# Splitting 128 rows per partition 64/64 instead of 65/63 in a two-group gate-and-dispatch kernel

## The chip, the cores and the metric

The kernel runs on one core of one Trainium2 chip. The metric is the device time of one execution in microseconds (us). Six runs of the kernel before gave a median of 240.24 us, from 240.06 to 240.39.

## The reference

For each of 16 x 1024 = 16,384 tokens there are eight router logits and a row of 512 floats (2 KB). The two largest softmax probabilities are taken and normalised against each other, and the row is written out twice, once multiplied by the smaller and once by the larger of the two weights:

```
probs = softmax(router_logits)
topk_indices = argsort(probs)[..., -2:]
topk_probs = take(probs, topk_indices);  topk_probs /= sum(topk_probs)
out = (x repeated k=2 times) * topk_probs[..., newaxis]     # [16, 1024, 2, 512] float32
```

So 33.55 MB of x and 0.52 MB of logits are read, and 67.11 MB of output are written. After normalising, the two weights are the sigmoids of minus and plus the difference of the two largest logits.

## The kernel before

The 16,384 tokens are put on 128 partitions, 128 tokens (called rows here) for each. They are cut into two groups by `GROUPS`: in the first, each partition has 65 successive rows of x, in the second 63. In the memory of the chip's DRAM the rows of one partition lie together, so neighbouring partitions are 65 x 2 KB = 130 KB apart in x and 65 x 4 KB = 260 KB apart in the output for the first group, and 126 KB and 252 KB for the second.

Three tiles in SBUF matter. `xs` has room for one group of rows (65 slots of 2 KB for each partition). `osp` holds the output of 16 rows (16 x 4 KB). `logits` holds all logits. `WA` holds both weights of each row.

For each group the SyncE queue (SP) first issues the loads of `LOADS[g]`, in rows: 2, 4, 2, 8, 17, 28, 4 for the first group and 16, 16, 31 for the second. The logits are loaded after the first six rows, and VectorE (DVE) works out the weights (lines 24 to 40, with two sigmoids on ScalarE in lines 42 and 43). Then a list named `plan` is worked through. Each entry is a first row, a number of rows and a place for the output; one multiplication on DVE (line 128) writes both copies, and one DMA (line 136) stores them. The entries of a group are:

- the first 16 rows into `osp` (in the first group as 2 rows, stored from ScalarE's queue, and 14 rows);
- rows 16 to 31 into slots 0 to 31 of `xs`, over rows that are no longer needed;
- rows 32 to 39 and 40 to 47 into the two halves of `osp`;
- the entries of `LAST[g]`, written over slots of `xs`: rows 48 to 56 and 57 to 64 in the first group, rows 48 to 62 in the second. The function `over` puts the output of row r into slots 2r - G and 2r - G + 1, where G is the number of rows of the group. For row 48 and G = 65 that is slot 31.

Everything on SP is in one order: the loads of group 0, the stores of group 0, the loads of group 1, the stores of group 1. A transfer that has to wait holds up all that stands behind it on SP. The framework puts in the waits: a load into slots of `xs` waits for the stores that read them, and a multiplication waits for the loads that it reads and for the stores that read what it overwrites.

A DMA over 128 partitions is shared by 16 DMA engines, eight partitions for each. In the trace's packet records each partition's stretch of a DMA is one packet: a store of 16 rows has 128 packets of 64 KB, a load of 28 rows 128 packets of 56 KB.

Of the kernel before, what the change touches and what calls it, by code (L numbers as in the profile page):

```python
# [1 line left out]

# [4 lines left out]

F32 = mybir.dt.float32
ALU = mybir.AluOpType
ACTF = mybir.ActivationFunctionType  # L10
P = 128


def top2_weights(nc, pool, logits, M, E, tag=""):

    hi, lo, n = None, None, E  # L20
    while n > 1:
        n //= 2
        if hi is None:
            a, b = logits[:, :, 0:n], logits[:, :, n : 2 * n]
            nhi = pool.tile([P, M, n], F32, tag=f"hi{n}{tag}")
            nlo = b
            nc.vector.tensor_tensor(nhi, a, b, op=ALU.max)  # L27
            nc.vector.tensor_tensor(nlo, a, b, op=ALU.min)  # L28
        else:
            a, b = hi[:, :, 0:n], hi[:, :, n : 2 * n]  # L30
            nhi = pool.tile([P, M, n], F32, tag=f"hi{n}{tag}")
            nlo = pool.tile([P, M, n], F32, tag=f"lo{n}{tag}")
            tmp = pool.tile([P, M, n], F32, tag=f"tmp{n}{tag}")
            nc.vector.tensor_tensor(tmp, lo[:, :, 0:n], lo[:, :, n : 2 * n], op=ALU.max)  # L34
            nc.vector.tensor_tensor(nlo, a, b, op=ALU.min)  # L35
            nc.vector.tensor_tensor(nlo, nlo, tmp, op=ALU.max)  # L36
            nc.vector.tensor_tensor(nhi, a, b, op=ALU.max)  # L37
        hi, lo = nhi, nlo
    dlt = pool.tile([P, M], F32, tag=f"dlt{tag}")
    nc.vector.tensor_tensor(dlt, hi[:, :, 0], lo[:, :, 0], op=ALU.subtract)  # L40
    WA = pool.tile([P, M, 2], F32, tag=f"WA{tag}")
    nc.scalar.activation(WA[:, :, 0], dlt, ACTF.Sigmoid, scale=-1.0)  # L42
    nc.scalar.activation(WA[:, :, 1], dlt, ACTF.Sigmoid, scale=1.0)  # L43
    return WA

GROUPS = [65, 63]

LOADS = [[2, 4, 2, 8, 17, 28, 4], [16, 16, 31]]


LAST = [[(48, 9), (57, 8)], [(48, 15)]]


@with_exitstack
def kernel(
    ctx: ExitStack,
    tc: tile.TileContext,  # L60
    x: bass.AP,
    router_logits: bass.AP,
    k: bass.AP,
    out: bass.AP,
):
    nc = tc.nc
    B, S, D = x.shape
    E = router_logits.shape[-1]
    N = B * S
    assert int(k) == 2 and E == 8 and N == P * sum(GROUPS)  # L70
    M = N // P

    L = 16
    x_v, o_v, rl_v = [], [], []
    t0 = 0
    for n in GROUPS:
        t1 = t0 + P * n
        x_v.append(
            x.rearrange("b s d -> (b s) d")[t0:t1].rearrange("(p m) d -> p m d", p=P)
        )  # L80
        o_v.append(
            out.rearrange("b s k d -> (b s) k d")[t0:t1].rearrange(
                "(p m) k d -> p m k d", p=P
            )
        )
        rl_v.append(
            router_logits.rearrange("b s e -> (b s) e")[t0:t1].rearrange(
                "(p m) e -> p m e", p=P
            )
        )  # L90
        t0 = t1

    wpool = ctx.enter_context(tc.tile_pool(name="wpool", bufs=1))
    logits = wpool.tile([P, M, E], F32)
    xs = wpool.tile([P, max(GROUPS), D], F32)
    osp = wpool.tile([P, L, 2, D], F32)

    def over(r, n, G):

        a = 2 * r - G
        return xs[:, a : a + 2 * n, :].rearrange("p (r k) d -> p r k d", k=2)

    h = L // 2
    e = 2
    m0 = 0
    for g, G in enumerate(GROUPS):
        r = 0  # L110
        for n in LOADS[g]:
            nc.sync.dma_start(xs[:, r : r + n, :], x_v[g][:, r : r + n, :])  # L112
            r += n
            if g == 0 and r == 6:

                nc.sync.dma_start(logits[:, :G], rl_v[0])  # L116
                nc.sync.dma_start(logits[:, G:], rl_v[1])
                WA = top2_weights(nc, wpool, logits, M, E)
        assert r == G
        begin = [(0, e, osp[:, :e]), (e, L - e, osp[:, e:])] if g == 0 else [(0, L, osp)]  # L120
        plan = begin + [
            (L, L, over(L, L, 2 * L)),
            (2 * L, h, osp[:, :h]),
            (2 * L + h, h, osp[:, h:]),
        ]
        plan += [(r, n, over(r, n, G)) for r, n in LAST[g]]
        for r, n, og in plan:
            nc.vector.tensor_tensor(  # L128
                og,
                xs[:, r : r + n, :].unsqueeze(2).to_broadcast([P, n, 2, D]),  # L130
                WA[:, m0 + r : m0 + r + n, :].unsqueeze(3).to_broadcast([P, n, 2, D]),
                op=ALU.mult,
            )

            queue = nc.scalar if n == e else nc.sync
            queue.dma_start(o_v[g][:, r : r + n], og)  # L136
        m0 += G


# [1 line left out]
_INS = ['x', 'router_logits', 'k']  # L141
_OUTS = [((16, 1024, 2, 512), 'float32')]

_NUMBERS = {'k': 2}


# [26 lines left out]
```

## Time and profile before

| What | Value |
|---|---|
| Median of six runs | 240.24 us (240.06 to 240.39) |
| The profiled execution's own time | 240.09 us |
| Its span in the profile | 238.3 us, so 1.8 us lie outside of it |
| DVE busy | 142.0 us (60%) |
| DMA moved | 101.19 MB, mean 425 GB/s |
| Busy share of the 16 DMA engines | 97.8% for SP's queue (q1) and 1.0% for ScalarE's (q10) |

The span is cut into 40 slices, and a digit gives the busy share of a slice in tenths. A "wait" row says which instruction waited, on what, for how long. SP is not a computing engine here; "SPq" is its queue of issues. The figures of the DMA share are sums of packet times as a share of 16 engines' span.

### The profile page before, as it was taken

To read this page: it belongs to the slowest core of one execution; us is meant where nothing else is said; L and a number is where in the kernel's file an instruction comes from. 1 tells how busy PE (TensorE), PEld (TensorE's weight loads), DVE (VectorE), ACT (ScalarE), POOL (GpSimd) and SP (SyncE) were. 2 spreads that over 40 slices of the span, in tenths; PEclk is the share of its full clock that TensorE was granted. 3 is DMA by queue.
4 is the path that set the end of the run, shared out by engine and by line. 5 is a ranking of instruction groups with operands and counts; after the bars stand their busy time and mean duration, and the time that the engine had idled before them with its cause. 6 is when DMAs were issued, how large, how long until landed. Compare 5 with 4: busy or idle time off the path is not lost.

```text
span 238.3 us, 117 instructions
## 1 busy us (share of the span) xinstructions
DVE 142.0 (60%) x23; ACT 1.8 (1%) x3; POOL 0.2 (0%) x4
## 2 busy tenths in 40 slices
DVE  0599999900299699900000699999106999990000
ACT  2000000000000000000000000000000000000000
POOL 0000000000000000000000000000000000000000
DMA  6999999899798999999999999998998989999995
GB/s 250 435 481 386 446 488 462 330 462 462 341 517 352 440 440 440 440 402 478 434 429 423 402 506 405 448 484 385 429 451 385 495 352 440 440 440 429 495 443 217
DMA packets 3456, 101.19 MB, mean 425 GB/s; under 512 B 384, under 2 KB 512, under 8 KB 896
## 3 DMA queue, kind: packets, MB, share of 16 engines
q1 hardware_dynamic: 3312, 100.14, 97.8%
q10 hardware_dynamic: 144, 1.05, 1.0%
HBM read 34.08 MB, written 67.11 MB: 425 GB/s over the span
## 4 chain that ended last, share of the span: by engine, by line
DMA 43%; DVE 41%; issue 4%; SPq 1%; ACT 0%; DVEq 0%
DVE xs L128 22%; DVE osp L128 18%; DMA out_dram<-xs 15%; DMA xs<-in_x_dram 13%; DMA out_dram<-osp 13%; DMA logits<-in_router_logits_dram 3%; SPq L112 0%; DVE nhi L27 0%; DVE logits L28 0%; DVE nlo L36 0%; DVE tmp L34 0%; DVE nhi L37 0%; DVE nlo L35 0%; SPq L116 0%; SPq L136 0%
## 5 line engine op out<-in xcount | busy, mean ns | idle before, releaser
L128 DVE TENSOR_TENSOR osp<-xs,WA 128x8192 f32<-128x8192 f32 (+3 forms) x7 | 69.1, 9908 | 61.9 <-DMA xs<-in_x_dram 31.2
L128 DVE TENSOR_TENSOR xs<-xs,WA 128x16384 f32<-128x16384 f32 (+3 forms) x5 | 69.1, 13811 | 2.2 <-DMA out_dram<-xs 2.0
L27 DVE TENSOR_TENSOR nhi<-logits 128x512 f32<-128x512 f32 x1 | 0.7, 692 | 8.3 <-DMA logits<-in_router_logits_dram 8.3
L42 ACT ACT_TABLE_LOAD x1 | 1.3, 1283 | 0.7 <-PEq L154 0.7
L28 DVE TENSOR_TENSOR logits<-logits 128x512 f32<-128x512 f32 x1 | 0.7, 691 | 0.0
L35 DVE TENSOR_TENSOR nlo<-nhi 128x256 f32<-128x256 f32 (+1 forms) x2 | 0.7, 350 | 0.0
L36 DVE TENSOR_TENSOR nlo<-nlo,tmp 128x256 f32<-128x256 f32 (+1 forms) x2 | 0.7, 350 | 0.0
L37 DVE TENSOR_TENSOR nhi<-nhi 128x256 f32<-128x256 f32 (+1 forms) x2 | 0.7, 349 | 0.0
L34 DVE TENSOR_TENSOR tmp<-logits 128x256 f32<-128x256 f32 x1 | 0.4, 417 | 0.0
L42 ACT ACTIVATE WA<-dlt 128x128 f32<-128x128 f32 x1 | 0.3, 315 | 10.2 <-DVE dlt L40 10.2
L40 DVE TENSOR_TENSOR dlt<-nhi,nlo 128x128 f32<-128x128 f32 x1 | 0.3, 292 | 0.0
L43 ACT ACTIVATE WA<-dlt 128x128 f32<-128x128 f32 x1 | 0.3, 299 | 0.0
L34 DVE TENSOR_TENSOR tmp<-nlo 128x128 f32<-128x128 f32 x1 | 0.3, 282 | 0.0
L154 POOL MEMSET const-bfloat16-1.0<- 128x1 bf16 x1 | 0.1, 102 | 0.0
L154 POOL MEMSET const-uint8-127<- 128x1 uint8 x1 | 0.1, 101 | 0.0
L154 POOL MEMSET const-float32-0.0<- 128x1 f32 x1 | 0.1, 99 | 0.2 <-issue 0.2
L154 POOL MEMSET const-float32-1.0<- 128x1 f32 x1 | 0.1, 98 | 0.0
## 6 DMA issues: line engine op xcount, KB each, us to landing
out_dram<-osp SPq DMA_DIRECT2D x4, 4096.0 KB, 20.7
xs<-in_x_dram SPq DMA_DIRECT2D x2, 4096.0 KB, 30.0
xs<-in_x_dram SPq DMA_DIRECT2D x1, 7936.0 KB, 37.8
out_dram<-xs SPq DMA_DIRECT2D x1, 7680.0 KB, 23.1
xs<-in_x_dram SPq DMA_DIRECT2D x1, 7168.0 KB, 39.6
out_dram<-osp SPq DMA_DIRECT2D x1, 7168.0 KB, 33.8
out_dram<-xs SPq DMA_DIRECT2D x1, 4608.0 KB, 20.4
xs<-in_x_dram SPq DMA_DIRECT2D x1, 4352.0 KB, 22.6
```

The costliest lines, as they stand in the source:

```text
L27: nc.vector.tensor_tensor(nhi, a, b, op=ALU.max)
L28: nc.vector.tensor_tensor(nlo, a, b, op=ALU.min)
L34: nc.vector.tensor_tensor(tmp, lo[:, :, 0:n], lo[:, :, n : 2 * n], op=ALU.max)
L35: nc.vector.tensor_tensor(nlo, a, b, op=ALU.min)
L36: nc.vector.tensor_tensor(nlo, nlo, tmp, op=ALU.max)
L37: nc.vector.tensor_tensor(nhi, a, b, op=ALU.max)
L40: nc.vector.tensor_tensor(dlt, hi[:, :, 0], lo[:, :, 0], op=ALU.subtract)
L42: nc.scalar.activation(WA[:, :, 0], dlt, ACTF.Sigmoid, scale=-1.0)
L43: nc.scalar.activation(WA[:, :, 1], dlt, ACTF.Sigmoid, scale=1.0)
L128: nc.vector.tensor_tensor(og, xs[:, r : r + n, :].unsqueeze(2).to_broadcast([P, n, 2, D]), WA[:, m0 + r : m0 + r + n, :].unsqueeze(3).to_b ...
L154: nc = _bacc.Bacc("TRN2", target_bir_lowering=False, num_devices=1)
```

## The change

The two groups get 64 rows each, so neighbouring partitions are 128 KB apart in x and 256 KB apart in the output in both groups. The first group is loaded in pieces of 2, 4, 2, 8, 16 and 32 rows (six instead of seven), the second in 16, 16 and 32. The last 16 rows of each group are one multiplication and one store; with G = 64 their output goes into slots 32 to 63. `xs` has 64 slots instead of 65. The loop is untouched.

```diff
+GROUPS = [64, 64]
 
-GROUPS = [65, 63]
-
-LOADS = [[2, 4, 2, 8, 17, 28, 4], [16, 16, 31]]
+LOADS = [[2, 4, 2, 8, 16, 32], [16, 16, 32]]
 
 
-LAST = [[(48, 9), (57, 8)], [(48, 15)]]
+LAST = [[(48, 16)], [(48, 16)]]
```

## The prediction

> **What bounds the kernel now.** I read the profile's page first: the engines' busy times, the row of DMA shares, the queues.
>
> ```profile
> DVE 142.0 (60%) x23; ACT 1.8 (1%) x3; POOL 0.2 (0%) x4
> ...
> DMA  6999999899798999999999999998998989999995
> ...
> q1 hardware_dynamic: 3312, 100.14, 97.8%
> q10 hardware_dynamic: 144, 1.05, 1.0%
> ```
>
> The reader is to see that no computing engine is near full and that the 16 DMA engines are: 97.8 + 1.0 = 98.8% of 238.3 us is 235.4 us of packets on each. The packet records say where the missing 2.9 us lie: the first data packet starts at 1.97 us and the last one ends at 237.35 us. Those ends are 235.4 us apart, so between them the engines never run dry. The time is therefore the packet time plus 2.9 us at the ends plus the 1.8 us outside the span. The profiled execution took 240.09 us; the median is 0.15 above it. I sum differences on the profiled execution and lay them on the median.
>
> The waits come next, DVE's and SP's, and then the timeline.
>
> ```profile
> DVE osp L128 <- DMA xs<-in_x_dram: 31.2, 1, 31.2
> DVE osp L128 <- DMA out_dram<-osp: 30.1, 2, 16.7
> ...
> DVE xs L128 <- DMA out_dram<-xs: 2.0, 1, 2.0
> ```
>
> ```profile
> SPq L112 <- DMA out_dram<-xs: 20.0, 2, 10.3
> ...
> SPq L112 <- DMA xs<-in_x_dram: 2.4, 2, 2.1
> ```
>
> ```profile
> 64.02 17.30 DVE L128 TENSOR_TENSOR osp<-xs,WA 128x8192 f32<-128x8192 f32 x2 [16.70 <-DMA out_dram<-osp]
> 72.73 8.94 SPq L136 DMA_DIRECT2D out_dram<-osp  x2
> 83.36 18.48 DVE L128 TENSOR_TENSOR xs<-xs,WA 128x9216 f32<-128x9216 f32 x2 [2.05 <-DMA out_dram<-xs]
> 93.14 9.06 SPq L136 DMA_DIRECT2D out_dram<-xs  x2
> ...
> 180.90 17.29 DVE L128 TENSOR_TENSOR osp<-xs,WA 128x8192 f32<-128x8192 f32 x2 [13.40 <-DMA out_dram<-osp]
> ...
> 214.42 0.33 SPq L136 DMA_DIRECT2D out_dram<-xs  x1
> ```
>
> All these waits are of engines waiting for a DMA queue that is full. A wait removed is worth nothing unless the queue would have run dry. So two questions decide: does the packet time change, and does the queue run dry anywhere in the new order?
>
> **Packet time from sizes.** In the packet records a packet's duration depends on its size almost alone. Medians in ns: 8 KB 309, 32 KB 1213, 34 KB 1288, 36 KB 1364, 56 KB 2116, 60 KB 2267, 62 KB 2342, 64 KB 2418. From 32 to 64 KB that is 37.7 ns per KB and 8 ns per packet. Each DMA gives an engine eight packets.
>
> - Removed: loads of 17, 28, 4 and 31 rows (34, 56, 8, 62 KB): 10.30 + 16.93 + 2.47 + 18.74 us. Stores of 9, 8 and 15 rows (36, 32, 60 KB): 10.91 + 9.70 + 18.14 us. Sum 87.19 us.
> - Added: a load of 16 rows (32 KB) 9.70, and two loads of 32 rows and two stores of 16 rows, all of 64 KB packets: 4 x 19.34. Sum 87.08 us.
> - Two DMAs fewer also means two closing packets of 9 ns fewer for each engine, 0.02 us.
>
> Together -0.13 us. Bytes are the same, so nothing else in this term can move. That a load is cut into 64 KB packets is not shown (the largest load packet is 62 KB; 64 KB ones occur in stores); loads and stores of 56 KB have the same median, 2116 ns, so I take the store's figure. Cut in two it would cost 8 x 8 ns more.
>
> **The 4-row load.** One of the removed loads was dearer than its size. The 4-row load at the end of group 0 took a mean of 370 ns per packet, from 309 to 745, between 43.5 and 46.9 us; the other 4-row load, near the start, a mean of 309. The excess is 8 x 61 ns = 0.49 us on each engine, in the path. In the new kernel its rows are part of a 32-row load. The nearest row is the last load of group 1 (31 rows, mean 2345 against 2342), with an excess of 0.02 us. But the cause is not to be seen, and a stutter of DRAM reads at that moment would hit whatever load is running. So the term lies between 0 and -0.48; I take -0.24, since of the two loads with 8 KB packets one had the whole excess and one none.
>
> **The queue in the new order.** Group 0 loads end 0.6 us earlier (64 rows), and all that follows shifts with them; I keep the old clock.
> - DVE's 2.05 us wait at 83.36 existed because row 48's output began in slot 31, which the store of slots 0 to 31 still read. It now begins in slot 32, so the wait goes. DVE runs 64.02 + 17.30 + 17.23 (the 16-row multiplication, from its two rows of 17.22 and 17.23) = 98.6 us until the last store of group 0 is issued, where the first of two pieces was issued at 93.14. The queue needs it at 102.0, when the first packet of the old piece started. Slack 3.4 us, from 8.9.
> - The second load of group 1 waited for that same slot 31 until 113.5; now it goes out at once, behind the first. The third still waits, for the whole last store, to about 122 us, with two loads of 9.7 us queued ahead of the engines. That 19.4 us is the cover; gone, the gap would be about the 1.24 us from the first issue (0.73) to the first packet (1.97). Behind the waiting SP stands only the store issued near 149, so nobody is held up.
> - The last store of all is issued at 180.90 + 17.29 + 17.23 = 215.4 instead of 214.42; its packets are needed at 218.7. Slack 3.3 us, from 4.3.
> - SP's 2.1 us wait before the ninth transfer falls away with that transfer; SP's next issue is at 30.09, so nothing follows.
> - DVE's instruction for 9 and 8 rows (18.48 together) becomes 17.23, its last 16.16 becomes 17.23. Both only use slack.
>
> With 1.24 us from issue to packet the queue stays full. The sum is -0.13 - 0.24 = -0.37 us: 239.72 on the profiled execution, 239.87 on the median. Its own range is 239.63 to 240.11, the two ends of the 4-row term.
>
> **A rule against the change.** Before, partitions lay 130 or 126 KB apart in x and 260 or 252 KB in the output; 128 and 256 KB are powers of two. The trace shows no such pitch. It does show that doubling the pitch, from 130 KB (load of 28 rows) to 260 KB (store of 14 rows), leaves 56 KB packets at 2116 ns, so I put the cost at nothing in the sum. The Trainium skill, "DMA: Bandwidth & Descriptors", section "Latency and other measured facts", says that copies whose partitions lie a large power of two apart in HBM lose rate, 207 GB/s at 512 KiB and 103 at 4 MiB where the padded pitch gives 214. No run here shows it. An estimate by that page: the loss at 512 KiB, 3.3%, would make about 8 us of 235.4; our pitches are smaller by 2 and 4, so less. The sum by the row stays 239.87.
>
> **Rivals.**
> 1. *The power-of-two pitch slows the packets* (slower). For it: 16 engines run nearly in step, so their addresses would differ by multiples of the pitch. Against it: medians and minima of the large packets agree within a few ns, so the engine's own rate sets them, and DRAM has to fall below that before any time is lost. Price by rows: at least nothing; the mildest disturbance seen is the 17-row load beside ScalarE's store, 1297 against 1288 ns (0.7%), the strongest the 4-row load's 370 against 309 (20%). All large packets are the undisturbed kind, so I stay near the mild row: 0.7% of 235.4 is 1.65 us, less 0.37, gives 241.5. It decides as soon as 64 KB packets pass 2432 ns, their largest so far. Chance 0.24.
> 2. *The last store comes too late* (slower). ScalarE's store was issued at 15.09 and its first packet started at 18.86, 3.8 us later, among busy engines. If a store on SP needs as long, slacks of 3.4 and 3.3 us leave gaps of 0.4 and 0.5 us, and with the 0.37 gained the time is 240.8. Against it: that was another queue, which had to fall in behind packets already taken up. It decides where the slack falls below the time from issue to packet. Chance 0.06.
> 3. *The whole excess of the 4-row load goes* (faster): -0.13 - 0.48 gives 239.63. For it, the last load of group 1; against it, the unknown cause. Chance 0.24, with all that lies below 239.76.
>
> The sum's case, with rates as they are and the excess partly back, has the remaining 0.46.
>
> **How the numbers follow.** A measurement can tell about 0.2% here, 0.48 us: faster is below 239.76, slower above 240.72. Faster is rival 3, 0.24. Slower is rivals 1 and 2, 0.30. The rest is 0.46. The range goes down to 239.55, just past rival 3, and up to 242.5, past rival 1's price; the dearer half of the pitch case, about 0.12, is left out above, and 0.05 below.
>
> **What would show it.** Right: DMA share near 98.8%, first packet near 2.0 and no gap inside; 64 KB packets at 2418 ns for loads and stores alike; DVE's wait for the store from xs gone; the third load of group 1 issued near 122. Wrong by rival 1: medians above 2432 and 1213 ns. By rival 2: an idle stretch of the DMA before the last store of a group. By rival 3: last load of group 0 with no packet above its size's median.

## The result: slower by 0.4%

The changed kernel took 241.09 us (median of 18 runs, 240.62 to 242.42), beside 240.26 us (36 runs, 239.96 to 240.90) for the kernel before. The ratio is 1.0039, with a 95% interval of 1.0029 to 1.0048. The forecast was 239.87 us.

The profiled execution of the change took 240.75 us, its span is 239.0 us. It lies 0.34 below its own median, so the profile shows 0.66 of the 0.83 us. The page's rows that answer to those of before, the busy times, the slices and the queues:

```profile
DVE 141.8 (59%) x22; ACT 1.8 (1%) x3; POOL 0.2 (0%) x4
...
DMA  7999998899989799999989998989999898999894
...
q1 hardware_dynamic: 3024, 100.14, 97.8%
q10 hardware_dynamic: 144, 1.05, 1.0%
```

The queue is as full as before, in a longer span: the same bytes took more packet time. DVE's waits, SP's waits and the timeline of the change:

```profile
DVE osp L127 <- DMA xs<-in_x_dram: 33.5, 1, 33.5
DVE osp L127 <- DMA out_dram<-osp: 30.2, 2, 16.2
```

```profile
SPq L111 <- DMA out_dram<-xs: 21.8, 1, 21.8
...
SPq L135 <- DMA xs<-in_x_dram: 2.1, 1, 2.1
```

```profile
63.56 17.30 DVE L127 TENSOR_TENSOR osp<-xs,WA 128x8192 f32<-128x8192 f32 x2 [16.21 <-DMA out_dram<-osp]
...
80.89 17.23 DVE L127 TENSOR_TENSOR xs<-xs,WA 128x16384 f32<-128x16384 f32 x1
98.14 0.33 SPq L135 DMA_DIRECT2D out_dram<-xs  x1
98.53 23.87 SPq L111 DMA_DIRECT2D xs<-in_x_dram  x3
131.62 17.23 DVE L127 TENSOR_TENSOR osp<-xs,WA 128x16384 f32<-128x16384 f32 x1 [33.51 <-DMA xs<-in_x_dram]
...
180.14 17.29 DVE L127 TENSOR_TENSOR osp<-xs,WA 128x8192 f32<-128x8192 f32 x2 [14.03 <-DMA out_dram<-osp]
...
214.72 0.33 SPq L135 DMA_DIRECT2D out_dram<-xs  x1
```

The reader is to see that the order did what was foretold: the row of DVE's wait for a store from `xs` (2.0 us before) is gone; DVE goes from one multiplication to the next at 80.89 with no wait, the last store of group 0 is issued at 98.14, and SP waits once for a store from `xs`, 21.8 us, before the third load. Nor does the queue run dry: the packet records show fewer than 16 packets under way only at the two ends.

Where the time went, from packet records (a packet's *excess* is what it took beyond the median for its size, summed and divided by 16 engines):

| us per engine | before | change |
|---|---|---|
| first load (2 rows) | 0.53 | 0.60 |
| load of rows 16 on, beside ScalarE's store | 0.07 | 0.22 |
| last load of group 0, before its stores | 0.49 | 0.57 |
| last store of group 0, before the loads of group 1 | 0.00 | 0.14 |
| first two loads of group 1 | 0.05 | 0.12 |
| last load of group 1, before its stores | 0.02 | 0.22 |
| all packets | 1.20 | 1.89 |

0.69 us more excess, less the 0.13 us that the sizes save, comes near the 0.57 us by which the stretch from first packet to last grew (235.38 to 235.95 us). The sum is of the mean engine and the slowest one sets the stretch (it ended 0.29 us behind the mean before, 0.38 in the change), so that it comes out so closely is partly chance. 0.13 us more lies behind the last landing (below). The excess does not lie on all packets: medians are 2418 ns for 64 KB, loads and stores alike. Most of it lies where loads and stores meet: on 16 packets, the last of each engine, of the load that ends at 46.2 us, of the store that ends at 121.3, and of the load that ends at 160.4.

(The packet times in the prediction were read against a start 0.23 us too early. The first packet starts at 1.74 us, 1.0 us after its issue, and the slacks were 3.2 and 3.1 us. No step turns on it.)

### The profile page after: what moved, and what is told of

Its sections match the earlier page's. It is cut to its first block, busy times and chain, and to the rows that moved or that the text cites. A ratio compares the mean times of both kernels' runs of the same rounds, so it can differ in the third digit from the quotient of the medians.

```text
span 239.0 us, 112 instructions
## 1 busy us (share of the span) xinstructions
DVE 141.8 (59%) x22; ACT 1.8 (1%) x3; POOL 0.2 (0%) x4
## 4 chain that ended last, share of the span: by engine, by line
DMA 43%; DVE 41%; issue 4%; SPq 1%; ACT 0%; DVEq 0%
DMA out_dram<-osp 27%; DVE osp L127 25%; DVE xs L127 14%; DMA xs<-in_x_dram 14%; DMA logits<-in_router_logits_dram 3%; SPq L111 0%; DVE nhi L27 0%; DVE logits L28 0%; DVE nlo L36 0%; DVE nhi L37 0%; DVE nlo L35 0%; DVE tmp L34 0%; SPq L115 0%; SPq L135 0%; ACT WA L42 0%
## 5 line engine op out<-in xcount | busy, mean ns | idle before, releaser
L127 DVE TENSOR_TENSOR xs<-xs,WA 128x16384 f32<-128x16384 f32 x4 | 68.9, 17225 | 0.1
```

The lines of the kernel that those rows point to most:

```text
L127: nc.vector.tensor_tensor(og, xs[:, r : r + n, :].unsqueeze(2).to_broadcast([P, n, 2, D]), WA[:, m0 + r : m0 + r + n, :].unsqueeze(3).to_b ...
```

## Experiments

The theories at the start: 1, reads 128 KB apart; 2, the sizes of the pieces; 3, stores 256 KB apart. Ratios are to the kernel before on the same chip, with 95% intervals.

**e1: the change with reads 130 KB apart.** The view of x has 65 rows for each partition; 64 are read.

```diff
+        rd = 65
+        c0 = min(t0, N - P * rd)
         x_v.append(
-            x.rearrange("b s d -> (b s) d")[t0:t1].rearrange("(p m) d -> p m d", p=P)
+            x.rearrange("b s d -> (b s) d")[c0 : c0 + P * rd].rearrange(
+                "(p m) d -> p m d", p=P
+            )
```

> The changed kernel, but x is read with 65 rows (130 KB) between partitions in both groups; it reads other rows than the reference wants, as many and in the same pieces; stores stay 256 KB apart. Theory 1 (reads 128 KB apart lose time wherever stores are in flight beside them): the extra time goes, 240.1 us, ratio to the kernel before 0.998 to 1.0005, and the last packets of group 0's 32-row load are back near 2418 ns (they were 2830 to 3212). Theory 2 (64 KB load packets and one-piece stores): stays at 241.1 us, ratio 1.004. Theory 3 (stores 256 KB apart): also stays at 241.1.

Measured 241.03 us, 1.0034 (1.0021 to 1.0047), and 0.65, 0.21 and 0.40 us of excess at the three switches. Theory 1 alone fails.

**e5: the kernel before with reads 128 KB apart.** The view of x has 64 rows for each partition and the load's first row is `min(r, 64 - n)`.

> The kernel before with all its pieces and stores, but x read with 64 rows (128 KB) between partitions (the last row of group 0 is read from one row too low, so that it fits; sizes are as before). Theory 1: slower by what the change cost, 240.9 to 241.2 us, ratio 1.003 to 1.004. Theory 2 and theory 3: 240.26 us, ratio 1.000.

Measured 240.26 us, 1.0004 (0.9992 to 1.0016). Theory 1 fails here too.

**e2: the kernel before with a 32-row load.**

```diff
-LOADS = [[2, 4, 2, 8, 17, 28, 4], [16, 16, 31]]
+LOADS = [[2, 4, 2, 8, 17, 32], [16, 16, 31]]
```

> The kernel before with its last two loads of group 0 (28 and 4 rows) joined to one of 32 rows, so 64 KB load packets at 130 KB between partitions. Theory 1: no loss, 239.8 to 240.3 us; if the 4-row load's 0.49 us was due to its small packets, 239.8, if it belongs to the switch from loads to stores, 240.2. Theory 2: slower, 240.6 us. Theory 3: 240.2.

Measured 240.32 us, 1.0010 (0.9997 to 1.0023). With the 4-row load gone its excess stayed: the 32-row load that took its place has 0.52 us, on each engine's last packet. So the prediction's -0.24 us was nothing: the excess belongs to the switch from loads to stores, whatever packet is there.

**e3: the change with small pieces.** Loads 2, 4, 2, 8, 16, 28, 4 and 16, 16, 28, 4; last pieces of 9 and 7 rows in both groups.

> The changed kernel (64 and 64 rows, 128 and 256 KB between partitions) with small pieces as before: the 32-row loads cut into 28 and 4 rows, the last stores into 9 and 7 rows. Theory 1 and theory 3 (distance between partitions): stays near 241.1 us, ratio 1.004. Theory 2 (sizes): back at 240.3, ratio 1.000.

Measured 241.30 us, 1.0038 (1.0026 to 1.0050): as slow as the change. Theory 2 fails.

**e6: the kernel before with stores 256 KB apart.** The output views have 64 rows for each partition; the last store of group 0 is cut. The lines of the views and the `else` with the old store are left out here ("...").

```diff
...
+            if r + n > 64:
+                queue.dma_start(o_v[0][:, r:64], og[:, : 64 - r])
+                queue.dma_start(o_v[1][:, 63:64], og[:, 64 - r :])
...
```

> The kernel before with its groups, loads and multiplications, but its output rows stored 64 rows (256 KB) apart in both groups; the 65th row of each partition is stored by a DMA of its own into the free place of the second half (output rows stand elsewhere, as many are written). That DMA of 4 KB packets costs 0.06 us by packet sizes. Theory 3 (stores 256 KB apart): 241.0 to 241.3 us, ratio 1.003 to 1.004, with the excess of load packets at the switches between loads and stores in group 1 above 0.2 us. Theory 4 (the distance does not matter, it is the equal split itself: how the pieces' ends fall against each other): 240.3 us, ratio 1.000.

Measured 240.44 us, 1.0008 (1.0000 to 1.0017). The loads at the two switches of group 1 have 0.26 us of excess (0.07 in the kernel before), the sign that theory 3 named, but the time moved by less than it expected.

**e7: the change with stores 260 and 252 KB apart.** As in e6 the other way round: the views are cut at row 65 x 128, and the last row of group 1 goes into the free place of the first view.

> The changed kernel with its groups, loads and multiplications, but its output rows stored 65 rows (260 KB) apart in the first half and 63 rows (252 KB) apart in the second, as in the kernel before; the last row of each partition is stored by a DMA of its own into the free place of the first half (output rows stand elsewhere). It costs 0.06 us by packet sizes. Theory 3: 240.2 us, ratio 0.999 to 1.001, and the excess at the switches in group 1 back under 0.1 us. Theory 4: stays at 241.1 us, ratio 1.004.

Measured 240.80 us, 1.0017 (1.0005 to 1.0029), its runs from 240.10 to 241.40. Half of the loss is gone. The excess at the switches of group 1 did not go as theory 3 expected: the last store's packets are back at their median, but the last load of group 1 has 0.49 us, more than in the change.

**e8: both distances doubled.** One view of 128 rows for each partition, of which a group takes 64. The edit of x is shown; output and logits have the same one ("...").

```diff
-            x.rearrange("b s d -> (b s) d")[t0:t1].rearrange("(p m) d -> p m d", p=P)
+            x.rearrange("b s d -> (b s) d").rearrange("(p m) d -> p m d", p=P)[
+                :, c0 : c0 + n
+            ]
...
```

> The changed kernel with both groups taken from one layout of 128 rows for each partition, so that x is read 256 KB apart and the output is stored 512 KB apart; pieces and order are those of the change. Theory 3: more loss than at 256 KB, above 241.3 us; an estimate by the Trainium skill's 3.3% at 512 KiB would be about 248 us. Theory 4: 241.1 us, as the change.

Measured 242.44 us, 1.0093 (1.0080 to 1.0106). Pieces and order are those of the change, so the distances did it, those of reads and stores together. The timeline says where:

```profile
63.32 17.29 DVE L130 TENSOR_TENSOR osp<-xs,WA 128x8192 f32<-128x8192 f32 x2 [16.08 <-DMA out_dram<-osp]
...
132.75 17.22 DVE L130 TENSOR_TENSOR osp<-xs,WA 128x16384 f32<-128x16384 f32 x1 [34.89 <-DMA xs<-in_x_dram]
...
181.67 17.29 DVE L130 TENSOR_TENSOR osp<-xs,WA 128x8192 f32<-128x8192 f32 x2 [14.43 <-DMA out_dram<-osp]
```

Between the first two rows the queue moves stores of 16, 8, 8 and 16 rows and a load of 16: 19.34 + 9.70 + 9.70 + 19.34 + 9.70 = 67.78 us by sizes. The rows are 69.43 us apart, 1.65 too many; the change's rows of the same kind (63.56 and 131.62) are 0.28 too many. In that stretch lies the one switch from stores to loads, and the packets agree: 1.0 us of excess on the last packets of the store, 0.64 on the first load behind it.

The 3.3% at 512 KiB that the prediction estimated from the Trainium skill's rates for copies between tensors in HBM ("DMA: Bandwidth & Descriptors", "Latency and other measured facts") is not what this kernel pays at that store distance: 0.9%.

**e9: the kernel before with all stores on SP.** Line 135 reads `queue = nc.sync`.

> The kernel before with its first store (2 rows) on SP's queue, behind the loads, instead of ScalarE's, so that no store runs beside the loads of group 0. If the mix of loads and stores costs what the excess of the load packets between 14 and 26 us shows (0.07 us in the kernel before, 0.22 in the changed one): 240.1 to 240.2 us, ratio 0.9995. If the excess at the end of group 0's loads (0.49 us) comes from the first stores to the output in general, it stays there; if it comes from the store on the other queue, it goes: 239.7.

Measured 240.46 us, 1.0008 (1.0000 to 1.0017). The excess of the 17-row load fell from 0.07 to 0.03 us, that of the last load of group 0 stayed at 0.53. So that one does not come from ScalarE's queue, and the mix of queues is not worth removing.

**e10: the change with both distances off the power of two (e1 and e7 together).**

> The changed kernel with its groups and pieces, but both sides off the power of two: x read 130 KB apart, output stored 260 and 252 KB apart, the last row of each partition by a DMA of its own (other rows are read and the output rows stand elsewhere; as many). Theory 5 (reads and stores both count: where one side or the other lies a power of two apart, the switch between loads and stores costs more, most where both do): ratio 0.999 to 1.001, 240.0 to 240.4 us, excess at the switches of group 1 under 0.1 us. Theory 4 (the equal split or its pieces, not the distance): 241.0 us, ratio 1.003 to 1.004.

Measured 240.48 us, 1.0013 (1.0003 to 1.0024): most of the loss gone, a rest left. The excess at the switches of group 1 is 0.20 us, where theory 5 expected under 0.1.

**e11: the kernel before with both at 128 and 256 KB (e5 and e6 together).**

> The kernel before with its groups and pieces, but both sides at a power of two: x read 128 KB apart and output stored 256 KB apart, the 65th row of each partition by a DMA of its own (0.06 us). Theory 5: slower, 240.9 to 241.2 us, ratio 1.003 to 1.004, with 0.2 us or more of excess at the switches of group 1. Theory 4: as with only the stores moved, 240.4 us, ratio 1.0005.

Measured 240.66 us, 1.0019 (1.0008 to 1.0031): slower, by half of what the change costs.

**e12: the change again.**

> The changed kernel once more, beside the two others on the same chip. Both theories: 241.1 us, ratio 1.003 to 1.005; a second look at where its packets' excess stands: over 0.2 us at the switches of group 1, and 0.12 us more between the last landing and the end than in the kernel before.

Measured 240.88 us, 1.0033 (1.0019 to 1.0047); excess at the switches 0.36, 0.15 and 0.36 us, and 0.94 us behind the last landing again.

**e13: groups of 63 and 65.** `GROUPS = [63, 65]`, loads 2, 4, 2, 8, 16, 31 and 16, 17, 32, last pieces 15, and 9 and 8.

> The kernel before with its groups the other way round, 63 and then 65 rows (loads 2, 4, 2, 8, 16, 31 and 16, 17, 32; last pieces 15, and 9 and 8), so that no distance is a power of two and the order and sizes of the pieces are new. Theory 5: 240.1 to 240.5 us, ratio 0.999 to 1.001. Theory 4, if what counts is how the pieces fall against each other: anything from 240.2 to 241.1 us.

Measured 240.73 us, 1.0022 (1.0006 to 1.0038), its runs from 240.18 to 242.25. Neither distance is a power of two, so something else counts as well. In the slow kernels so far the last load of group 0 had large packets (e3 and e11 excepted), which gave theory 6. Four kernels test it.

**f1: e10 with the 32-row load of group 0 cut into 28 and 4.**

> The kernel with the changed pieces and distances of 130 and 260 KB (ratio 1.0013), with the 32-row load of group 0 cut into 28 and 4 rows; other rows are read and the output rows stand elsewhere, as there. Theory 6 (a small last load before the switch keeps the engines together): ratio 1.000, 240.2 us, the slowest engine at the end under 0.35 us behind the mean (it was 0.6 to 0.9). Theory 7 (the last load's size does not matter): 1.0013, 240.5 us.

Measured 240.33 us, 1.0002 (0.9991 to 1.0014). The time is back, though this interval and that of e10 overlap; and the slowest engine still ended 0.7 us behind the mean, not under 0.35, so the reason that theory 6 gives did not show.

**f2: e13 with its 31-row load cut into 27 and 4.**

> The split of 63 and 65 rows (ratio 1.0022) with its 31-row load of group 0 cut into 27 and 4 rows. Theory 6: 240.2 us, ratio 0.9995 to 1.001. Theory 7: 240.7 us, ratio 1.002.

Measured 240.60 us, 1.0020 (1.0011 to 1.0030). Theory 6 fails here; the runs are only closer together (240.27 to 241.24).

**f3: the change with its 32-row load of group 0 cut into 28 and 4.**

```diff
-LOADS = [[2, 4, 2, 8, 16, 32], [16, 16, 32]]
+LOADS = [[2, 4, 2, 8, 16, 28, 4], [16, 16, 32]]
```

> The changed kernel with only its 32-row load of group 0 cut into 28 and 4 rows, distances 128 and 256 KB as in the change. Theory 6: a part goes, 240.7 us, ratio 1.002, what the distances cost. Theory 7: 241.0 us, ratio 1.0035.

Measured 241.07 us, 1.0045 (1.0027 to 1.0064): no better than the change.

**f4: the kernel before with a second small last load (16, 16, 27, 4).**

> The kernel before with the 31-row load of group 1 cut into 27 and 4 rows as well. Theory 6: no slower than the kernel before, 240.0 to 240.2 us, ratio 0.999 to 1.000, and the engines as close after the second switch as after the first. Theory 7: 240.2 us, ratio 1.000.

Measured 240.27 us, 1.0004 (0.9995 to 1.0012). Nothing gained; of the kernels run none came out faster than the one before.

f1 and f3 differ in the distances, and in the DMA of its own for the last row that f1 needs. Two more kernels complete the square, each with f1's and f3's pieces.

**f5: e7 with the cut load (reads 128, stores 260 and 252 KB apart).**

> The pieces of f1 and f3, with x read 128 KB apart as in the change and the output stored 260 and 252 KB apart (output rows stand elsewhere). If the stores' distance is what counts: as f1, ratio 1.000 to 1.001. If the reads' distance counts: as f3, 1.003 to 1.005. If both have a share: about 1.002.

Measured 240.49 us, 1.0013 (1.0005 to 1.0022).

**f6: e1 with the cut load (reads 130, stores 256 KB apart).**

> The pieces of f1 and f3, with x read 130 KB apart (other rows are read, as many) and the output stored 256 KB apart as in the change. If the stores' distance is what counts: as f3, ratio 1.003 to 1.005, with the last packets of group 0's last store above 2450 ns. If the reads' distance counts: 1.000. If both have a share: about 1.002.

Measured 241.35 us, 1.0042 (1.0030 to 1.0054).

The square, with the mean duration of 16 packets, the last of each engine, in group 0's last store (the median for 64 KB is 2418 ns):

| reads, stores apart | ratio | these packets |
|---|---|---|
| f1: 130, 260 KB | 1.0002 | 2418 ns |
| f5: 128, 260 KB | 1.0013 | 2420 ns |
| f6: 130, 256 KB | 1.0042 | 2569 ns |
| f3: 128, 256 KB | 1.0045 | 2547 ns |

With the 32-row load uncut it is the same: 2421 (e10) and 2418 ns (e7) at 260 KB, 2556 (change), 2572 (e12) and 2626 ns (e1) at 256 KB, and 3423 ns (e8) at 512 KB. All other packets of that store are at 2418 in all of these. The timeline's rows of e8's kind, the second being the multiplication that waits for the first load behind that store, in f1, f5, f6 and f3:

```profile
63.73 17.29 DVE L131 TENSOR_TENSOR osp<-xs,WA 128x8192 f32<-128x8192 f32 x2 [16.28 <-DMA out_dram<-osp]
...
131.48 17.22 DVE L131 TENSOR_TENSOR osp<-xs,WA 128x16384 f32<-128x16384 f32 x1 [33.20 <-DMA xs<-in_x_dram]
```

```profile
63.46 17.29 DVE L128 TENSOR_TENSOR osp<-xs,WA 128x8192 f32<-128x8192 f32 x2 [16.09 <-DMA out_dram<-osp]
...
131.43 17.23 DVE L128 TENSOR_TENSOR osp<-xs,WA 128x16384 f32<-128x16384 f32 x1 [33.42 <-DMA xs<-in_x_dram]
```

```profile
63.75 17.30 DVE L131 TENSOR_TENSOR osp<-xs,WA 128x8192 f32<-128x8192 f32 x2 [16.14 <-DMA out_dram<-osp]
...
132.00 17.23 DVE L131 TENSOR_TENSOR osp<-xs,WA 128x16384 f32<-128x16384 f32 x1 [33.69 <-DMA xs<-in_x_dram]
```

```profile
63.95 17.30 DVE L127 TENSOR_TENSOR osp<-xs,WA 128x8192 f32<-128x8192 f32 x2 [16.34 <-DMA out_dram<-osp]
...
132.00 17.23 DVE L127 TENSOR_TENSOR osp<-xs,WA 128x16384 f32<-128x16384 f32 x1 [33.50 <-DMA xs<-in_x_dram]
```

The rows are 67.75 and 67.97 us apart with stores 260 KB apart, 68.25 and 68.05 with 256 KB: 0.3 us more. The packets say the same. The excess of the last store of group 0 and the two loads behind it is 0.02 and 0.07 us (f1, f5; 0.06 and 0.08 in e10 and e7), against 0.42 and 0.28 (f6, f3; 0.26, 0.29 and 0.38 in the change, e12 and e1).

A mean over the square: stores at 256 KB instead of 260 cost 1.0044 - 1.0008 = 0.36%, reads at 128 instead of 130 KB 1.0029 - 1.0022 = 0.07%, no more than the intervals allow for chance. The change, e1, e7 and e10 are the same square with the change's own pieces. There stores at 256 KB cost 0.22% (change and e7) and 0.21% (e1 and e10), reads at 128 KB 0.05 and 0.04%. Over both squares the stores' distance costs 0.29%, 0.7 us; one pair alone is uncertain by 0.15 to 0.2%. The 260 KB kernels have a DMA more, 0.06 us by sizes, and one wait fewer behind the end, 0.06 us; the two cancel.

## Why the prediction failed

**The bound and the order held.** The queue is full from first packet to last, the waits changed as said (but SP's 2.1 us wait did not fall away: it stands before the first store now, and costs nothing there either), the last store of each group came in time (issued at 214.72, its first packet at 217.69). Rival 2 did not happen. 64 KB load packets take 2418 ns, as taken from the stores, so the term of sizes stands at -0.13 us.

**The step that failed is the one called "A rule against the change".** It put the cost of the distances at nothing, because 56 KB packets had one duration at 130 and 260 KB. That row shows a stream under way, and it was right about streams: at 128 and 256 KB, even at 512, packets inside a stream keep their medians. It could not speak about the switches. With the change's own pieces the term is +0.2%, 0.5 of the 0.83 us; with the 32-row load cut it is 0.36%, 0.86 us. It is the stores' distance; reads alone cost nothing that can be told (e5, 1.0004). With the pieces of before it is less: 1.0008 (e6) and 1.0019 (e11). The traces place some 0.27 us of it, at the switch from stores to loads.

**Rival 1 had the distance right and the place wrong.** It gave 241.5 us by letting all packets slow by 0.7%, with medians above 2432 ns as the sign. The sign did not come, and the price was too high: packets in mid-stream did not slow. That 241.09 us lies within the range is owed to this price, which was laid on a slowing that did not happen. The row of the Trainium skill that the prediction cites ("DMA: Bandwidth & Descriptors", "Latency and other measured facts") pointed the right way, for a distance below those that it lists.

**The 4-row load's term (-0.24 us) was nothing.** Its reasoning "of the two loads with 8 KB packets one had the whole excess and one none" compared sizes; what differed was the neighbour. The prediction had the other end as well, a stutter that would hit whatever load is running, and that end was right. Every kernel run here has 0.31 to 0.65 us of excess at the end of group 0's loads, at any size and distance. Rival 3 fell with it.

**A term was missing.** In the end SP waits for its DMA semaphores one after another in a fixed order (each step 0.06 us), and two DMAs fewer put the last store on a semaphore that comes earlier in that order, with more waits behind it. From the last landing to the end the trace has 0.81 us before and 0.94 in the change. This is 0.13 us of the 0.83, and undoes what the sizes saved. With the 0.5 us of the stores' distance, about 0.3 us of the 0.83 is left.

**What stays open.** How the stores' distance lengthens the last packets at a switch was not seen; that memory gets many engines' first writes or reads at like addresses is an idea only. Nor are those packets the whole of its cost: in e3 the last store before the loads has 28 KB packets, the last of each engine took 1074 ns beside 1062, 0.01 us, and e3 is as slow as the change. The excess of the last load of group 1 does not follow the distance (0.49 us in e7 with 260 KB and in f3 with 256, 0.04 in f1 with 260). Only 256 and 512 KB were set against 252 and 260, so that it must be a power of two is not shown. With both distances off it, the change's pieces still cost 0.13% (e10), about 0.3 us, and the 63 and 65 split is slower by 0.2% (e13, f2) with no power of two in it; no run explains these. Nor does any explain the 0.5 us at the end of group 0's loads.

## What to carry to other kernels

In a kernel whose DMA queue is full throughout, look for time at the switches between loads and stores, not in the streams: packet durations there, beside the median for their size, show what a mean rate hides. A distance between partitions, here 256 KB between stores, can cost at the switches while the packets in mid-stream keep their durations; a split that is a row off, as here 65 and 63, may be doing work that no wait in the profile shows. Price such a distance by a kernel that moves it alone, with the pieces that the change has: with other pieces it cost from 0.1 to 0.4% here. When an odd row in a trace is dear, ask what stands beside it before pricing its removal.

## What the runs showed of the hardware beyond what was expected

- Store to load: the last 64 KB packet of each engine takes 2418 to 2421 ns with stores 260 KB apart, 2547 to 2626 at 256 KB and 3423 at 512 KB (where reads were 256 KB apart too).
- Load to store costs too: 0.31 to 0.65 us for each engine at the first switch in every kernel.
- Engines did not draw level again within a stream. In e2 the slowest engine was 0.82 us behind the mean of the 16 after the first switch, 1.49 after the third, and still 1.49 at the end; its profiled run took 241.41 us where its median is 240.32. The runs' scatter (240.62 to 242.42 us for the change) is of the same size; that such a lag makes it was not shown.
